# Turning attention's probabilities through DRAM (VectorE's 32x32 blocks, GpSimd's stores, a reload) in place of TensorE transposes

## The chip, the cores and the metric

The kernel runs on one core of a Trainium2 chip. The metric is the device time in microseconds of one execution. A run's time is a little longer than the span of its profile, which goes from the first instruction of the program to the last.

## The reference

One layer of a hybrid decoder is computed in float32 for a prompt of 1024 tokens and for 8 samples of 4 tokens each. The input is normalised and modulated, then multiplied by one wide matrix. Two branches follow: an mLSTM with 4 heads (a matrix memory, worked in chunks of 128 tokens) and a sliding-window attention with 8 query heads, 2 key heads, a head size of 64, a window of 128 and a learned sink per head. Gates merge the branches, an output matrix and a residual follow, and a last normalisation. The change touches the attention of the prompt alone:

```python
def sink_attend(q, k, v, q_pos, k_pos, sinks):
    ...
    s = jnp.einsum('bnqkgd,bnskd->bnkgqs', qg, k.astype(f32)) * (A_HEAD_DIM ** -0.5)
    ...
    s = jnp.where(mask[None, :, None, None], s, -jnp.inf)
    ...
    mx = jnp.maximum(jnp.max(s, axis=-1, keepdims=True), sink)
    p = jnp.exp(s - mx)
    den = jnp.sum(p, axis=-1, keepdims=True) + jnp.exp(sink - mx)
    o = jnp.einsum('bnkgqs,bnskd->bnqkgd', p / den, v.astype(f32))
```

Each block of 128 queries attends to the 128 keys of its own block and the 128 of the block before.

## The kernel before

**The main stream.** TensorE works through a list of jobs: the projections of keys and values, then four query groups (`aq`), eight inputs of the mLSTM heads (`mq`, `mk`, `mv` of heads 0 and 1 and two of head 2), and after them paired products (`block_products`) for the rest of the wide matrix: the other head inputs, the branch gates, the gates of attention and of the heads. The output matrices come last. Operands are split into a high and a low part, and each 128x128 step is three matmuls. The weights of a job are loaded one or two jobs ahead through SyncE's queue.

**The side streams.** All else that is computed meanwhile is written as Python generators that a planner, `Side`, weaves into the matmuls while the program is built. It keeps a clock, `side.now`, that each matmul moves on by its planned time. A generator issues some instructions and then yields a lag and the PSUM banks that its next step needs; the step is placed when the lag is over and the banks (`a`, `b`, `o`) have been left alone long enough (`HOLD`), and steps that need banks keep 1.5 us apart from the last one that issued products (`quiet`). The order on TensorE is fixed by this; on the chip the engines then wait for each other by semaphores. If an operand is late there, the whole of TensorE's queue stands behind it. Each stream has a limit of generators that are live at once and a least gap between their starts: `m` (the gate computations, then one generator `head(h)` per mLSTM head) 2 and 35 us; `a` (turning keys and values, then the 16 attention units) 5 and 8 us; `x` (sums of blocks for the paired products, loads) 2; `s` (attention of the samples, then `sample_head(h)`, four of them, added when head 3 has ended) 1; `g` 1. Where the main stream may not go on before side work has been placed, `hook` calls `side.until`: the first paired product waits for `sum_blocks`, the gates of attention for all 16 units (`units_done`), and the gate of head h, at its product 6, for sample head h.

**A unit.** `unit(g, b0)` (lines 806 to 874) is the attention of query group g (one query head of each of the 2 key heads) for the two query blocks b0 and b0 + 1. Queries, rotated keys and values come from DRAM (`qD`, `kD`, `vnD`), into two tiles `uqv` and `ukv` that also hold the values. Its steps are: load; scores into two banks and, on VectorE, mask and maximum into `p` (queries on the partitions, up to 256 keys by 2 blocks for each key head); the exponentials on ScalarE; the scaling by 1/den, for one key head on VectorE and for the other on ScalarE; the turn of `p`, so that keys come to the partitions, as six (in the units with b0 = 0) or eight transposes of 128x128 on TensorE into bank `b` and two copies back into `p`, one on ScalarE and one on VectorE; the product with the values into bank `o`; a copy and a store into `oD`. Between them stand lags of 12, 2.5, 3, 7 and 5 us.

**Two places that turn data in another way.** `across` (line 1021) turns keys and values of the mLSTM heads, and `stage_c3` (line 1118) the outputs of the heads: VectorE's `transpose` turns each 32x32 block in place, and four DMAs issued by GpSimd, one for 32 partitions, store the blocks so that the DRAM tensor holds the whole turned tile. Each run of such a store is 32 numbers, 128 bytes.

**Tiles.** Almost all of the streams' tiles in SBUF, 2 KB a partition, come from one pool of 43 (`ht`). All loads and stores of the side streams, the weights among them, go through SyncE's queue in the order in which they were written; stores are put off by 4 us of the planner's clock (`store`).

Of the kernel before, what the change touches and what calls it, by code (L numbers as in the profile page):

```python
# [111 lines left out]
class Side:  # L112
# [4 lines left out]
    def __init__(self, each, limits, quiet):  # L117
        self.each, self.free = each, {}
        self.now, self.last, self.quiet, self.products = 0.0, 0.0, quiet, 0
        self.streams = {n: {"max": m, "gap": g, "wait": [], "live": [], "next": 0.0} for n, (m, g) in limits.items()}  # L120

# [17 lines left out]
    def tick(self):  # L139
        self.each()  # L140
        for st in self.streams.values():
            if st["wait"] and len(st["live"]) < st["max"] and self.now >= st["next"]:
                self.begin(st)
        used, visit = set(), self.now >= self.last + self.quiet
        for item in sorted((i for st in self.streams.values() for i in st["live"]), key=lambda i: i[1]):
            banks = set(item[2])
            if self.now < item[1] or used & banks or (banks and not visit) or any(self.now < self.free.get(b, 0) for b in banks):
                continue
            used |= banks
            for b in banks:  # L150
                self.free[b] = self.now + (6.0 if "+" in banks else HOLD[b])
            n = self.products
            self.step(item)
            if self.products > n:
                self.last = self.now
# [17 lines left out]
def body(tc, a):  # L173
    nc = tc.nc
    with ExitStack() as ctx:
# [65 lines left out]
        def dma(out, in_, late=False):  # L241
            stores(in_.tensor)
            issue(out, in_, late)

        def issue(out, in_, late=False):
            ins = nc.sync.dma_start(out, in_)
            ins = getattr(ins, "ins", ins)
            if late:
                no_sync(ins, free)
                free.clear()  # L250
            free.append(ins)

        side = Side(stores, {"m": (2, 35.0), "a": (5,8.0), "x": (2, 0.0), "s": (1, 0.0), "g": (1, 0.0)}, 1.5)
        def mm(out, lhsT, rhs, start, stop, share=1, more=False):
# [552 lines left out]
        def unit(g, b0):  # L807
            sink = at["sink"]
            los = [128 if b == 0 else 0 for b in (b0, b0 + 1)]
            n0 = 1 if b0 == 0 else 0  # L810
            qv, kv_ = ht([128, 4, 128], "uqv"), ht([128, 4, 128], "ukv")
            q, kT = qv[:, 0:2].rearrange("p c e -> p (c e)"), kv_[:, 0:3].rearrange("p c e -> p (c e)")
            vn = kv_[:, 3], qv[:, 2], qv[:, 3]
            dma(q, qD[g][:, b0 * 128:b0 * 128 + 256])
            dma(kT[:, n0 * 128:], kD[:, (b0 - 1 + n0) * 128:(b0 + 2) * 128])
            dma(qv[:, 2:4], vnD[:, b0:b0 + 2])
            if b0:
                dma(vn[0], vnD[:, b0 - 1])
            yield 12.0, sc_bank[1]
            p = [ht([128, 2, 256], f"p{kv}") for kv in range(2)]  # L820
# [25 lines left out]
            for kv in range(2):  # L846
                for i, lo in enumerate(los):
# [3 lines left out]
                    else:  # L851
                        V.tensor_scalar(p[kv][:, i, lo:], p[kv][:, i, lo:], den[:, j:j + 1], None, op0=ALU.mult)
            yield 7.0, "b"
            pT = [t.rearrange("p i (j e) -> p (i j) e", e=128) for t in p]
            for kv in range(2):
                pt = pb([128, 4, 128], f"pt{g}_{b0}_{kv}")
                for j in range(n0, 4):
                    tr(pt[:, j], p[kv][:, j // 2, j % 2 * 128:j % 2 * 128 + 128], ident)
                if kv:
                    V.tensor_copy(pT[kv][:, n0:], pt[:, n0:])  # L860
                else:
                    S.copy(pT[kv][:, n0:], pt[:, n0:])
            yield 5.0, "o"
            oT = po([128, 2, 128], f"oT{g}_{b0}")
            for j in range(n0, 4):
                i, hf = divmod(j, 2)
                for kv in range(2):
                    r = slice(64 * kv, 64 * kv + 64)
                    mm(oT[r, i], vn[i + hf][:, r], pT[kv][:, j], start=(hf == 0 or b0 + i == 0), stop=(hf == 1))
            c0 = b0 * 128  # L870
            o = qv[:, 0:2].rearrange("p c e -> p (c e)")
            S.copy(o, oT.rearrange("p c e -> p (c e)"))
# [148 lines left out]
        def across(h, n, src, c0):  # L1021
            m = src.shape[1]
            t = ht([128, 512], f"{n}t")[:, :m]
            V.transpose(t, src)
            for b in range(0, 128, 32):
                nc.gpsimd.dma_start(mN[n][h][c0:c0 + m, b:b + 32].rearrange("(t p) e -> p t e", p=32), t[b:b + 32].rearrange("p (t e) -> p t e", e=32))  # L1026

        def head(h):
# [89 lines left out]
            def stage_c3(p):  # L1118
# [7 lines left out]
                for b in range(4):  # L1126
                    nc.gpsimd.dma_start(yhD[h][c0:c0 + m].rearrange("c (q i) (b e) -> b i c q e", i=32, e=32)[b], by_block(y[32 * b:32 * b + 32]))  # L1127

# [606 lines left out]
        def hook(n, i):  # L1735
# [11 lines left out]
            if (n, i) == (len(pairs) - 1, 7):  # L1747
                prefetch(("w_ao", 0))
                gated(("w_ao", 0))

        LOADS = [(len(pairs) - 2, 7), (len(pairs) - 1, 6), (len(pairs) - 1, 7)]
        work = block_products(pairs, hook)
# [387 lines left out]
```

## Time and profile before

| | us |
|---|---|
| median of 3 runs | 859.94 |
| lowest and highest of them | 857.38, 860.94 |
| the profiled execution | 857.75 |
| its span | 855.9 |

In that span TensorE is busy for 822.3 us, VectorE for 604.1, ScalarE for 390.5 and GpSimd for 174.7; the mean granted TensorE clock is 0.992. The scores of the first unit start at 94.9 us, the product with values of the last unit at 274 us.

In the profile, PE is TensorE's matmuls and PEld its weight loads, DVE is VectorE, ACT ScalarE, POOL GpSimd, SP SyncE (SPq, its issuing of DMAs). A row of instructions by tile has the line, the engine, the operation, the tile written and the tiles read, the number of instructions, the duration of one in ns (least, median, most), the first and the last start in us, and the shapes. Most instructions carry the line of a helper (L219 for VectorE and ScalarE, L258 for matmuls, L263 for transposes, L246 for SyncE's DMAs), so the tile names tell them apart: `sc` are the scores, `p` the probabilities, `pt` the transposes in PSUM, `oT` the product with values. Rows of stages have the start and end, the length, the busy time of each engine with its number of instructions, the granted clock, the busy share of the 16 DMA engines and the GB/s that they moved.

### The profile page before, as it was taken

The numbers are of one execution on the slowest core, as the hardware profiler recorded it, in microseconds if no ns is written. First come the engines' busy times: TensorE is split into PE (matmuls) and PEld (weight loads), VectorE is DVE, ScalarE is ACT, GpSimd is POOL, SyncE is SP. The second block draws the span as 40 slices with busy tenths as digits, with TensorE's granted clock in tenths as the row PEclk, the third lists the DMA queues.
The fourth block names the chain that finished last, engine by engine and source line by source line (L and its number), as shares of the span: only waits on it lengthen the run. The fifth ranks groups of instructions, "written<-read, shape, count | busy, mean of one in ns | idle before, by whom it ended". The sixth has DMA issues, their size and how long they took to land. (4 is left out here: it accounts for less than half of the span.)

```text
span 855.9 us, 15332 instructions
## 1 busy us (share of the span) xinstructions
PE 822.3 (96%) x5139; PEld 686.6 (80%) x5139; DVE 604.1 (71%) x1596; ACT 390.5 (46%) x963; POOL 174.7 (20%) x236
## 2 busy tenths in 40 slices
PE   6899999999999989999999999999999999999984
PEld 3689988789789778888887777777788999967863
DVE  3787785555687778668666565978766669857987
ACT  4672356545564543555444454434443333233334
POOL 0220000330341434211111000000012032532563
PEclk9999999999999999999999999999999999999998
DMA  9995549459756765664444335553436974273322
GB/s 326 366 356 183 150 137 291 134 125 294 214 153 203 214 170 151 194 198 135 129 115 130 115 111 162 160 150 89 116 99 203 345 254 137 82 247 99 111 99 104
DMA packets 125347, 150.82 MB, mean 176 GB/s; under 512 B 29057, under 2 KB 81409, under 8 KB 125237
## 3 DMA queue, kind: packets, MB, share of 16 engines
q1 hardware_dynamic: 121044, 143.55, 53.5%
q0 software_dynamic: 4224, 6.30, 3.6%
q8 instruction: 40, 0.66, 0.3%
q14 instruction: 39, 0.31, 0.1%
HBM read 109.73 MB, written 41.08 MB: 176 GB/s over the span
## 5 line engine op out<-in xcount | busy, mean ns | idle before, releaser
L1127 POOL DMA_DIRECT2D yhD<-yt x48 | 28.9, 608 | 108.3 <-DVE yt L219 86.3
L258 PE MATMUL g_w_ao<-ya,wh_w_ao 128*128 128x384 f32 (+1 forms) x192 | 45.7, 322 | 0.1
L258 PE MATMUL g_w_mo<-ym_l,wh_w_mo 128*128 128x384 f32 (+1 forms) x192 | 45.7, 323 | 0.0
L219 ACT ACTIVATE p<-p,nmx 128x256 f32<-128x256 f32 (+1 forms) x64 | 31.0, 486 | 28.3 <-DVE nmx L219 28.3
L1026 POOL DMA_DIRECT2D mkN<-mkt x44 | 26.9, 618 | 45.5 <-DVE mkt L219 26.0
L219 DVE CUSTOM_DVE_ANT_0 p<-sc,cst,sink 128x256 f32<-128x256 f32 (+1 forms) x64 | 26.1, 463 | 11.4 <-PE sc L258 11.4
L258 PEld LDWEIGHTS g_w_ao<-ya,wh_w_ao 128*128 128x128 f32 x192 | 33.5, 188 | 0.7 <-DVE ya L219 0.6
L258 PEld LDWEIGHTS g_w_mo<-ym_l,wh_w_mo 128*128 128x128 f32 x192 | 33.5, 188 | 0.0
L258 PE MATMUL g_aq<-h_h,wh_aq 128*128 128x384 f32 (+1 forms) x96 | 32.5, 338 | 0.0
L1026 POOL DMA_DIRECT2D mvN<-mvt x40 | 24.7, 624 | 33.6 <-DVE mvt L219 12.5
L258 PE MATMUL g_aq<-h_l,wh_aq 128*128 128x384 f32 (+1 forms) x96 | 31.0, 323 | 0.0
L258 PE MATMUL g_w_mo<-ym_l,wl_w_mo 128*128 128x384 f32 (+1 forms) x96 | 31.0, 323 | 0.0
L258 PE MATMUL g_aq<-h_h,wl_aq 128*128 128x384 f32 (+1 forms) x96 | 31.0, 323 | 0.0
L258 PE MATMUL g_w_ao<-ya,wl_w_ao 128*128 128x384 f32 (+1 forms) x96 | 30.8, 321 | 0.0
L258 PE MATMUL g_mq<-h_h,wh_mq 128*128 128x384 f32 (+1 forms) x72 | 24.7, 344 | 0.8 <-ACT vs L219 0.8
L258 PE MATMUL g_mk<-h_h,wh_mk 128*128 128x384 f32 (+1 forms) x72 | 24.8, 344 | 0.0
L219 POOL TENSOR_TENSOR ya<-yr,ya 128x384 fp32r<-128x384 f32 (+1 forms) x6 | 7.3, 1222 | 80.7 <-DVE hg L219 67.4
L258 PE MATMUL g_mk<-h_l,wh_mk 128*128 128x384 f32 (+1 forms) x72 | 23.2, 323 | 0.0
L258 PE MATMUL g_mk<-h_h,wl_mk 128*128 128x384 f32 (+1 forms) x72 | 23.2, 323 | 0.0
L258 PE MATMUL g_mq<-h_h,wl_mq 128*128 128x384 f32 (+1 forms) x72 | 23.2, 322 | 0.0
L258 PE MATMUL g_mq<-h_l,wh_mq 128*128 128x384 f32 (+1 forms) x72 | 23.2, 322 | 0.0
L219 POOL COPY qs<-mk 128x32 f32<-128x32 f32 x3 | 1.4, 463 | 103.1 <-ACT mk L219 103.1
(1700 smaller groups left out, 2800.9 us busy)
## 6 DMA issues: line engine op xcount, KB each, us to landing
hb<-hD SPq DMA_DIRECT2D x24, 256.0 KB
x<-xT SPq DMA_DIRECT2D x16, 256.0 KB
early_h<-w_ada SPq DMA_DIRECT2D x8, 512.0 KB
hD<-x SPq DMA_DIRECT2D x16, 256.0 KB
adar_ga<-w_ada SPq DMA_DIRECT2D x16, 256.0 KB
wr_ga<-w SPq DMA_DIRECT2D x16, 256.0 KB
wr_gm<-w SPq DMA_DIRECT2D x16, 256.0 KB
taD<-gt SPq DMA_DIRECT2D x16, 256.0 KB
```

The source lines that it names most:

```text
L219: ins = f(*args, **kw)
L258: in_order(nc.tensor.matmul(out, lhsT, rhs, start=start, stop=stop, skip_group_check=more))
L1026: nc.gpsimd.dma_start(mN[n][h][c0:c0 + m, b:b + 32].rearrange("(t p) e -> p t e", p=32), t[b:b + 32].rearrange("p (t e) -> p t e", e=32))
L1127: nc.gpsimd.dma_start(yhD[h][c0:c0 + m].rearrange("c (q i) (b e) -> b i c q e", i=32, e=32)[b], by_block(y[32 * b:32 * b + 32]))
```

## The change

The transposes on TensorE and the copies out of PSUM go. Once `p` is scaled, the unit turns the 32x32 blocks of each key head's half with one VectorE instruction, into the tiles that held queries and keys (now `uq` and `uk`), and stores them with four GpSimd DMAs for each key head into a DRAM tensor `pD`, as `stage_c3` does. Some 12 us of the planner's clock later, SyncE loads `pD` into two new tiles `pT0` and `pT1`, and the values, which were loaded with the queries before, into `uv`. The product with the values follows and is the same as before; its copy goes into `pT0`. The lags of a unit are now 9, 2.5, 3, 3, 12 and 5, where 9, 12 and 5 are the least: `landed` makes them longer when the planner's count of DMAs issued on that queue (0.42 us each on SyncE, 0.65 on GpSimd) says that the queue is behind. Bank `b` is no longer used by units. The gap of stream `a` is 6.5 instead of 8 us. A new table `held` keeps stream `m` from starting a generator while another of it is live and fewer than 16 units are done. The stores of `across` and `stage_c3` go through the new `scatter`, which issues the same DMA and counts it.

```diff
@@ Side.tick
-        for st in self.streams.values():
-            if st["wait"] and len(st["live"]) < st["max"] and self.now >= st["next"]:
+        for name, st in self.streams.items():
+            held = name in self.held and self.held[name]()
+            if st["wait"] and not held and len(st["live"]) < st["max"] and self.now >= st["next"]:
                 self.begin(st)
@@ body
+        queue = {"sync": 0.0, "gpsimd": 0.0}
+
+        def put(eng, cost):
+            queue[eng] = max(queue[eng], side.now) + cost
+
+        def landed(eng, least):
+            return max(least, queue[eng] - side.now + (2.5 if eng == "sync" else 4.0))
+
+        def scatter(out, in_):
+            nc.gpsimd.dma_start(out, in_)
+            put("gpsimd", 0.65)
+
         def issue(out, in_, late=False):
             ins = nc.sync.dma_start(out, in_)
+            put("sync", 0.42)
...
-        side = Side(stores, {"m": (2, 35.0), "a": (5,8.0), "x": (2, 0.0), "s": (1, 0.0), "g": (1, 0.0)}, 1.5)
+        side = Side(stores, {"m": (2, 35.0), "a": (5, 6.5), "x": (2, 0.0), "s": (1, 0.0), "g": (1, 0.0)}, 1.5)
@@ unit
-            qv, kv_ = ht([128, 4, 128], "uqv"), ht([128, 4, 128], "ukv")
+            qv, kv_ = ht([128, 4, 128], "uq"), ht([128, 4, 128], "uk")
             q, kT = qv[:, 0:2].rearrange("p c e -> p (c e)"), kv_[:, 0:3].rearrange("p c e -> p (c e)")
-            vn = kv_[:, 3], qv[:, 2], qv[:, 3]
+            pD = [dp.tile([4, 128, 128], F32, name=f"pD{g}_{b0}_{kv}") for kv in range(2)]
             dma(q, qD[g][:, b0 * 128:b0 * 128 + 256])
             dma(kT[:, n0 * 128:], kD[:, (b0 - 1 + n0) * 128:(b0 + 2) * 128])
-            dma(qv[:, 2:4], vnD[:, b0:b0 + 2])
-            if b0:
-                dma(vn[0], vnD[:, b0 - 1])
-            yield 12.0, sc_bank[1]
+            yield landed("sync", 9.0), sc_bank[1]
...
-            yield 7.0, "b"
-            pT = [t.rearrange("p i (j e) -> p (i j) e", e=128) for t in p]
+            yield 3.0, ""
+            flat = lambda t: t.rearrange("p c e -> p (c e)")
+            for kv, t in enumerate((qv, kv_)):
+                V.transpose(flat(t)[:, n0 * 128:], flat(p[kv])[:, n0 * 128:])
+                for k in range(4):
+                    scatter(pD[kv][n0:].rearrange("c (q i) (k e) -> k i c q e", i=32, e=32)[k],
+                                        by_block(flat(t)[32 * k:32 * k + 32])[:, n0:])
+            yield landed("gpsimd", 12.0), ""
+            pT = [ht([128, 4, 128], f"pT{kv}") for kv in range(2)]
+            vn = ht([128, 4, 128], "uv")
             for kv in range(2):
-                pt = pb([128, 4, 128], f"pt{g}_{b0}_{kv}")
-                for j in range(n0, 4):
-                    tr(pt[:, j], p[kv][:, j // 2, j % 2 * 128:j % 2 * 128 + 128], ident)
-                if kv:
-                    V.tensor_copy(pT[kv][:, n0:], pt[:, n0:])
-                else:
-                    S.copy(pT[kv][:, n0:], pt[:, n0:])
-            yield 5.0, "o"
+                dma(pT[kv][:, n0:], pD[kv][n0:].rearrange("c p e -> p c e"))
+            dma(vn[:, n0:3], vnD[:, b0 - 1 + n0:b0 + 2])
+            yield landed("sync", 5.0), "o"
             oT = po([128, 2, 128], f"oT{g}_{b0}")
...
-            o = qv[:, 0:2].rearrange("p c e -> p (c e)")
+            o = flat(pT[0][:, 0:2])
@@ across (stage_c3 likewise)
-                nc.gpsimd.dma_start(mN[n][h][c0:c0 + m, b:b + 32].rearrange("(t p) e -> p t e", p=32), t[b:b + 32].rearrange("p (t e) -> p t e", e=32))
+                scatter(mN[n][h][c0:c0 + m, b:b + 32].rearrange("(t p) e -> p t e", p=32), t[b:b + 32].rearrange("p (t e) -> p t e", e=32))
@@ main stream
+        side.held["m"] = lambda: len(side.streams["m"]["live"]) > 0 and len(units_done) < 16
```

More of the change, by code (lines that the diff above doesn't have):

```diff
@@ L119, in __init__ @@
         self.now, self.last, self.quiet, self.products = 0.0, 0.0, quiet, 0
+        self.held = {}
         self.streams = {n: {"max": m, "gap": g, "wait": [], "live": [], "next": 0.0} for n, (m, g) in limits.items()}
@@ L868, in unit @@
                     r = slice(64 * kv, 64 * kv + 64)
-                    mm(oT[r, i], vn[i + hf][:, r], pT[kv][:, j], start=(hf == 0 or b0 + i == 0), stop=(hf == 1))
+                    mm(oT[r, i], vn[:, i + hf, r], pT[kv][:, j], start=(hf == 0 or b0 + i == 0), stop=(hf == 1))
             c0 = b0 * 128
-            o = qv[:, 0:2].rearrange("p c e -> p (c e)")
+            o = flat(pT[0][:, 0:2])
             S.copy(o, oT.rearrange("p c e -> p (c e)"))
@@ L1126, in stage_c3 @@
                 for b in range(4):
-                    nc.gpsimd.dma_start(yhD[h][c0:c0 + m].rearrange("c (q i) (b e) -> b i c q e", i=32, e=32)[b], by_block(y[32 * b:32 * b + 32]))
+                    scatter(yhD[h][c0:c0 + m].rearrange("c (q i) (b e) -> b i c q e", i=32, e=32)[b], by_block(y[32 * b:32 * b + 32]))
             for visit in ([(load, 0), 10.0, ""], [(prep, 0), 3.0, "o"], [(stage_e, 0), (stage_a, 0), 5.0, "o"],
```

## The prediction

> **What bounds the kernel now.** I read the page's busy shares first, then the busy time by stage, then the rows of the work that goes.
>
> ```profile
> span 855.9 us, 15332 instructions
> PE 822.3 (96%) x5139; PEld 686.6 (80%) x5139; DVE 604.1 (71%) x1596; ACT 390.5 (46%) x963; POOL 174.7 (20%) x236
> q1 hardware_dynamic: 121044, 143.55, 53.5%
> q0 software_dynamic: 4224, 6.30, 3.6%
> ```
>
> TensorE is busy 96% of the span. The last two lines are the DMA queues of SyncE and of GpSimd: packets, MB, share of 16 engines.
>
> ```profile
> core 0: us, PE busy (x) PEld busy (x) DVE busy (x) ACT busy (x) POOL busy (x), PEclk, DMA share, GB/s
> 0.00:65.00 65.00, 55.01 (x364) 37.75 (x367) 42.92 (x113) 39.72 (x67) 11.42 (x24) 1.00 0.97 347
> 85.00:205.00 120.00, 119.18 (x901) 104.27 (x900) 76.76 (x294) 61.28 (x197) 15.43 (x26) 1.00 0.61 179
> 205.00:285.00 80.00, 78.48 (x599) 69.45 (x598) 57.77 (x182) 42.22 (x128) 27.01 (x46) 1.00 0.71 199
> 285.00:310.00 25.00, 21.53 (x130) 17.59 (x129) 19.29 (x69) 12.34 (x34) 7.38 (x14) 0.93 0.78 223
> ```
>
> The attention units run between 85 and 285 us. There TensorE idles 2.3 of 200 us, so time taken out of its queue is time saved, as long as nothing that it then needs comes late. VectorE is busy 134.5 of the 200, ScalarE 103.5, GpSimd 42.4.
>
> **The change, part by part.**
>
> *The turn on TensorE goes.* Its rows, the waits of TensorE in this stage, and one visit in order of time:
>
> ```profile
> L263 PE MATMUL pt<-cst,p x120: 270/272/331, 111.2 to 260.4; 128*128 128x128 f32 x120
> L219 DVE COPY p<-pt x16: 539/684/692, 112.3 to 260.7; 128x512 f32<-128x512 f32 x12, 128x384 f32<-128x384 f32 x4
> L219 ACT COPY p<-pt x16: 458/568/595, 112.6 to 261.5; 128x512 f32<-128x512 f32 x12, 128x384 f32<-128x384 f32 x4
> ...
> PE bx L258 <- DVE f3r_w L219: 2.3, 1, 2.3
> PE pt L263 <- ACT p L219: 1.5, 2, 0.8
> PE bw L258 <- DVE t2l L219: 1.2, 1, 1.2
> ...
> 111.05 0.34 PE L258 MATMUL g_aq<-h_h,wl_aq 128*128 128x384 f32 x1
> 111.22 0.82 PE L263 MATMUL pt<-cst,p 128*128 128x128 f32 x6
> 111.80 0.42 PE L258 MATMUL g_aq<-h_h,wh_aq 128*128 128x384 f32 x1
> 112.06 0.34 PE L258 MATMUL g_aq<-h_l,wh_aq 128*128 128x384 f32 x1
> ```
>
> A transpose has a duration of 272 ns, but they are pipelined, so 120 x 0.272 = 32.6 us would count each more than twice. What one visit takes from the queue is read from the starts: the projection's matmuls follow each other every 0.17 us; six transposes hold the next one from 111.22 to 111.80, and its follower comes after 0.26 instead of 0.17. That is 0.58 + 0.09 = 0.67 us for six, 0.11 each, and 120 x 0.112 = 13.4 us in 16 visits. The 1.5 us in which the transposes waited for ScalarE's scaling of p go as well. Gain on TensorE: **14.9 us**. The copies out of PSUM leave ScalarE (16 x 0.57 = 9.1 us) and VectorE (16 x 0.68 = 10.9); neither bounds the stage, so I count nothing for them.
>
> *The blocks turned on VectorE.* 32 more instructions; the rows of the same operation and of the stores behind it are in the kernel already:
>
> ```profile
> L219 DVE STREAM_TRANSPOSE mkt<-mk x9: 439/570/580, 149.0 to 282.9; 128x384 f32<-128x384 f32 x6, 128x256 f32<-128x256 f32 x3
> L219 DVE STREAM_TRANSPOSE mkt<-mkv x2: 703/703/703, 329.6 to 337.7; 128x512 f32<-128x512 f32 x2
> L1026 POOL DMA_DIRECT2D mkN<-mkt x44: 582/617/782, 149.9 to 341.1; - x44
> mvN<-mvt POOLq DMA_DIRECT2D x16, 64.0 KB, 4.4
> mkN<-mkt POOLq DMA_DIRECT2D x24, 48.0 KB, 3.0
> ```
>
> 24 at 0.70 and 8 three-quarter ones at 0.57 make 21.4 us; less the 10.9 of the copies VectorE gets 10.5 us more work in a stage where it idles 65. Hidden, with one exception. Six of the 16 turns start after 205 us; their units put 6 x 0.65 = 4 us ahead of the block operands for the paired products, and at 285 to 310 TensorE already waits for VectorE (bx 2.3, bw 1.2 us above), while its own work up to there gets 6 x 0.9 = 5.4 us shorter. Between 0 and 5.4 us of the gain is lost at this edge; I take **2**, nearer to nothing because one of the two heads that share VectorE there is held back (below).
>
> *GpSimd's stores.* Eight per unit, 128 in all, 128 x 0.617 = 79 us of issue in a stage where GpSimd is free for 158 of 200. They share its queue with the key and value stores (four at a time, 2.5 us); a unit's store that comes behind them is late by that, and they by 4.9 us behind a unit's eight; their readers are loads planned far later. Hidden.
>
> *The new path of the operands.* Its stations come from these rows (scores, scaling, products; the two times after each row's durations are its first and last start):
>
> ```profile
> L258 PE MATMUL sc<-ukv,uqv x128: 272/376/481, 94.9 to 243.2; 64*128 64x256 f32 x112, 64*128 64x128 f32 x16
> L219 DVE TENSOR_SCALAR p<-p,den x32: 286/348/519, 102.2 to 251.0; 128x256 f32<-128x256 f32 x28, 128x128 f32<-128x128 f32 x4
> L258 PE MATMUL oT<-p,uqv x192: 272/273/324, 118.0 to 274.1; 128*64 128x128 f32 x192
> ```
>
> The first unit's scores start at 94.9 and its p is scaled 7.3 us later. From there: one transpose 0.7, eight issues 4.9, landing 3 to 4.4 (median rows above), so, with 0.9 for the scaling itself, the turned blocks are in DRAM 17 to 18 us after the scores, up to 21 behind other stores. The reload is two DMAs of 256 KB; the page gives no landing for SyncE's queue. The nearest rows are the 64 KB ones of GpSimd's, 4.4, and the transfer itself at 199 GB/s is 2.6 us, so I take 4 to 9. Operands ready: 21 to 30 us after the scores, say 25. The order of work places the products at 2.5 + 3 + 3 + 12 + 5 = 25.5 plus a wait for an "o" bank; that wait was, with a lag of 5, between 111.2 and 118.0 in the first unit 1.8 us and between 260.4 and 274.1 in the last 8.7, so about 5. The products stand at 30, the operands come at 25 with a spread of some 4: about one unit in eight waits, for 2 to 3 us, 0.3 us on the mean of 16. Cost **5 us** in all; between none and 16 x 4 = 64 if every operand comes at 29.5 and no bank is waited for. Behind a waiting product stands all of TensorE's queue, the projections above all, so each such microsecond counts whole. SyncE's queue waits for the stores before it issues the reload; behind it stand the next unit's loads, weights and the loads of block operands, which then start late by the same microseconds. It is issued 12 us after the transposes, when the chain above takes 9 to 10; I count nothing unless GpSimd has a backlog.
>
> The unit's loads lose one DMA (values come in one piece, and late), and the scores follow after 9 instead of 12 us. No TensorE wait for scores stands among those of before, so 3 us less margin is covered; bound 0 to 16 x 1, taken as nothing. At its end a unit holds three more tiles (the reloaded p and the values) of the 43 that all streams share, but gives back the two of p a dozen microseconds earlier; taken as nothing too.
>
> *DMA traffic.* The stores write 7.86 MB and the reloads read as much. By the share per MB of the two queue lines, 3.6/6.30 of 855.9 us and 53.5/143.55, the stores take 38 us of all sixteen engines and the reloads 25. The stage holds 0.61 x 120 + 0.71 x 80 = 130 us of packets now; 193 would be in 185. But packet times include standing behind others, and in bytes it is 37.4 + 15.7 = 53.1 MB in 185 us, 287 GB/s, where the first 65 us carried 347. Crowded, not full: I count it in the 5 us above. The Trainium skill, "DMA: Bandwidth & Descriptors", Specifications, says that a transfer needs at least 512 bytes for line rate and that below this the engine reads, modifies and writes. The trace agrees in direction: GpSimd's queue, whose stores are runs of 128 bytes, pays 78 us of packet time per MB against 51; had the stores cost what SyncE's do, they would be 25 us instead of 38.
>
> *The order of work.* The "m" stream now holds a second head while one is live and not all 16 units are done. Lags of a unit sum to 34.5 us against 29.5, but one bank wait of three is gone, so a unit lives about as long as before, and five still run side by side: I expect the 16th to end 0 to 10 us after its old place less the gain, 260 to 269.
>
> ```profile
> 250.56 1.39 SPq L246 DMA_DIRECT2D hq<-qD  x1
> 354.71 0.45 SPq L246 DMA_DIRECT2D hq<-qD  x1
> L219 DVE STREAM_TRANSPOSE yt<-et x12: 438/572/579, 246.3 to 450.0; 128x384 f32<-128x384 f32 x8, 128x256 f32<-128x256 f32 x4
> L263 PE MATMUL sty<-cst,sns x4: 242/243/244, 493.3 to 622.0; 32*128 32x32 f32 x4
> 640.13 0.39 PE L258 MATMUL bw<-t2h,wh_phead_gate__7542 128*128 128x512 f32 x1
> ```
>
> Head 1 started its loads at 250.56; its end let head 3 start at 354.71, which ended at 450; then the four sample heads follow one another and the last ends at 622.0. The last pair's product at 640.13 may not be placed before that: 18 us of slack. The gain moves 640 to about 632, so head 1 may be 10 us late. At 260 to 269 it is 9 to 18 late; without units beside it a head runs quicker. I take **1 us** lost, 0 to 8.
>
> *Sum:* the profiled execution took 857.75 us (1.9 outside the span); 857.75 - 14.9 + 2 + 5 + 1 = **850.9 us**. That execution is 2.2 below the median of the runs shown, and within their spread; I give 851.
>
> **Rivals.**
>
> *A. The operands come late in most units.* At 0.9 us per unit (landing 7 instead of 4, or SyncE behind its own waits) the gain is used up: 850.9 + 16 x 0.6 = 860.5, no change. For it: the longest landing on GpSimd's queue was 7.0 us. Against it: the "o" bank's wait gives 5 us of margin.
>
> ```profile
> DMA to landing us min/median/max: 2.0/3.6/7.0
> ```
>
> *B. The DMA engines fill up; slower.* Place: 85 to 285. If the packet times add as they stand, 193 us are needed, and at the highest share that a ten-microsecond window of the unit stage reached, 0.92 (below), the stage takes 210 instead of 200: 857.75 + 10 = 868. It decides as soon as the added traffic costs over 54 us by the packets' time (0.92 x 200 - 130). Against it: 347 GB/s was moved in the first stage.
>
> ```profile
> 135.00:145.00 10.00, 10.00 (x89) 8.95 (x86) 6.17 (x24) 6.16 (x19) 0.43 (x1) 1.00 0.92 301
> ```
>
> *C. The heads are held too long.* If the units end after head 0, head 1 starts about 40 us late, 30 of which reach 640: some 880.
>
> *D. GpSimd can't issue beside VectorE.* If each store had first to let one VectorE instruction of the length of a transpose pass, a unit's eight took 8 x (0.62 + 0.70) = 10.6 us instead of 4.9. The operands came at 31 us, behind the products at 30, and with the spread of 4 the mean wait were 2.1: 850.9 + 16 x 1.8 = 880. The trace speaks against it: the 44 key stores took 582 to 782 ns each, with VectorE 64 to 72% busy around most of them. The Trainium skill, "SBUF — State Buffer", Who interferes with whom, states such a lock (a store of GpSimd takes some 620 ns alone and 3100 beside a VectorE copy in a two-port mode). By that figure a unit's eight would take up to 25 us; no row here shows it.
>
> **How the numbers follow.** A measurement of this kernel tells about 0.5% (4.3 us) from no change. My forecast, 842 to 855: 0.60. A: 0.18. B: 0.10. C: 0.07. D: 0.03. Better than 842 (no waits at all, 843, and the wait at 285 gone too): 0.02. Faster 0.62, same 0.18, slower 0.20. The range 842 to 868 leaves out the better case, half of B, C and D, some 0.17; the likeliest case alone is 842 to 855.
>
> **What would show it.** Right: no transposes of p on TensorE, 32 more stream transposes near 0.7 us, 128 more GpSimd stores near 0.62, and TensorE's waits before the products with values summing to about 5 us; 285 us of before's work reached near 275. Wrong: those waits over 10 us (A); DMA share above 0.9 through the stage and waits on weights or block operands (B); TensorE idle near 630 ahead of the last pair (C). My weakest numbers are the reload's landing time and the end of the sixteenth unit.

## The result: 5% slower, and the profile after

The changed kernel takes 903.09 us (median of 4 runs, 901.48 to 908.11), the kernel before 859.5 beside it: 1.0519 times as long, 95% interval 1.0469 to 1.0569. The forecast was 851, with 868 as the upper end of its range. The profiled execution took 901.48 us.

The page of the changed kernel (lines as those shown of before):

```profile
span 899.7 us, 15403 instructions
PE 828.4 (92%) x5019; PEld 688.4 (77%) x5019; DVE 617.5 (69%) x1612; ACT 383.5 (43%) x947; POOL 254.5 (28%) x364
q1 hardware_dynamic: 135188, 151.42, 54.0%
q0 software_dynamic: 8320, 14.17, 7.1%
```

The 120 transposes are gone (5139 matmuls became 5019), 128 GpSimd instructions are new, and TensorE is busy for 6 us more than before: the same matmuls last longer. Its busy time and clock by stage:

```profile
85.00:205.00 120.00, 106.65 (x739) 91.70 (x739) 74.04 (x279) 49.23 (x163) 64.52 (x104) 0.93 0.79 211
205.00:285.00 80.00, 61.27 (x392) 51.23 (x391) 46.28 (x155) 33.17 (x109) 37.51 (x61) 0.87 0.80 227
285.00:310.00 25.00, 22.53 (x176) 21.00 (x175) 14.30 (x39) 8.27 (x24) 13.49 (x23) 0.93 0.81 214
```

Of the 200 us from 85 to 285 TensorE now idles 32 (before 2.3), and its granted clock has fallen from 1.00 to 0.93 and 0.87. The first paired product (`bx`), at 282.3 us before, starts at 320.7: 38 of the 44 us are lost by then. What it waits for between 85 and 330 us (total, times, longest):

```profile
PE oT L273 <- DMA uv<-vnD: 33.0, 9, 7.2
PE g_mq L273 <- DVE mvt L221: 5.0, 2, 3.2
PE g_mq L273 <- ACT mk L221: 0.4, 1, 0.4
PE oT L273 <- DMA qD<-mk: 0.2, 1, 0.2
```

33 us are the product with values waiting for its reloaded operands. The clock comes on top. Two short stretches of the changed kernel, each at or behind such a wait, and the only one of before in this part of the run:

```profile
136.80:143.60 6.80, 3.14 (x21) 2.84 (x22) 0.00 (x0) 0.37 (x1) 4.55 (x8) 0.50 1.08 346
280.10:283.50 3.40, 3.40 (x19) 2.96 (x19) 1.51 (x9) 2.54 (x11) 3.40 (x7) 0.50 0.60 189
```

```profile
302.40:305.80 3.40, 3.40 (x13) 2.93 (x12) 3.40 (x10) 1.24 (x2) 2.19 (x4) 0.50 0.84 245
```

The clock in them is 0.50. Between 85 and 330 us the changed kernel has nine such stretches of 3.4 or 6.8 us, one at or behind each of its nine waits of 1.8 us or more, and none by the two of 1.2 us. So such a wait is paid for again in part. The Trainium skill, "TensorE: Matmul & The Clock Gate", HAM oscillation, describes waits on DMAs that put the clock back to half; by its Part 1 that goes in windows of about 3.4 us, and the lengths here agree with it. The Trainium skill puts the limit there at idle gaps of about 3.4 us; here five waits of 1.8 to 3.2 us were enough.

What the clock costs is read from TensorE's busy time up to the first paired product (the rows 85.00:282.30 and 85.00:320.70 further below): an estimated 13.4 us of transposes are gone, and yet it is 2.0 us longer (196.97 against 194.96), so the slow stretches cost about 15. Together, 38.6 us of waits against 2.3 before and these 2.0 make 38, and the product is 38 late.

Why the operands come late is seen in one unit, in order of time (the changed kernel's timeline, engine by engine):

```profile
254.38 0.71 DVE L221 STREAM_TRANSPOSE uq<-p 128x512 f32<-128x512 f32 x1
255.02 0.67 DVE L221 STREAM_TRANSPOSE uk<-p 128x512 f32<-128x512 f32 x1
...
268.93 2.44 POOL L256 DMA_DIRECT2D mvN<-mvt  x4 [9.64 <-DVE mvt L221]
271.35 2.58 POOL L256 DMA_DIRECT2D pD<-uq  x4
273.93 2.57 POOL L256 DMA_DIRECT2D pD<-uk  x4
...
284.36 0.32 SPq L260 DMA_DIRECT2D oD<-pT  x1
284.86 0.98 SPq L260 DMA_DIRECT2D pT<-pD  x2
285.89 0.49 SPq L260 DMA_DIRECT2D uv<-vnD  x1
...
290.52 1.76 PE L273 MATMUL oT<-pT,uv 128*64 128x128 f32 x14 [2.22 <-DMA uv<-vnD]
```

The blocks are turned at 255.7; GpSimd stores them from 271.35, because in its queue they stand behind a value store that itself waited 9.6 us for VectorE; SyncE reloads them at 284.86, behind the store of the unit before (`oD`), which waits for that unit's product; and the product starts 4.6 us after the reload's last issue, 2.2 of them in TensorE's idle time. Three queues, each in a fixed order, take turns waiting for each other.

### The profile page after: what moved, and what is told of

It reads as the page before. It is cut to its first block, busy times and chain, and to the rows that moved or that the text cites. A ratio compares the mean times of both kernels' runs of the same rounds, so it can differ in the third digit from the quotient of the medians.

```text
span 899.7 us, 15403 instructions
## 1 busy us (share of the span) xinstructions
PE 828.4 (92%) x5019; PEld 688.4 (77%) x5019; DVE 617.5 (69%) x1612; ACT 383.5 (43%) x947; POOL 254.5 (28%) x364
## 5 line engine op out<-in xcount | busy, mean ns | idle before, releaser
L256 POOL DMA_DIRECT2D pD<-uq x64 | 40.8, 644 | 54.2 <-DVE uq L221 39.8
L273 PE MATMUL oT<-pT,uv 128*64 128x128 f32 x240 | 23.0, 349 | 33.3 <-DMA uv<-vnD 33.0
L273 PEld LDWEIGHTS oT<-pT,uv 128*64 128x64 f32 x240 | 18.2, 178 | 37.8 <-issue 27.8
L256 POOL DMA_DIRECT2D pD<-uk x64 | 41.0, 647 | 1.9 <-DMA mkN<-mkt 1.4
L273 PE MATMUL g_mq<-h_h,wh_mq 128*128 128x384 f32 (+1 forms) x72 | 27.4, 380 | 5.4 <-DVE mvt L221 5.0
L273 PE MATMUL g_mq<-h_l,wh_mq 128*128 128x384 f32 (+1 forms) x72 | 25.3, 352 | 0.0
```

Source lines behind the costliest of these rows:

```text
L256: nc.gpsimd.dma_start(out, in_)
L273: in_order(nc.tensor.matmul(out, lhsT, rhs, start=start, stop=stop, skip_group_check=more))
```

## The experiments

The theories, with the numbers or letters that the texts quoted below use: (1) the product stands too close behind its reload; (2) the added traffic; later split into (2a, then b) the DMA engines are full, runs of 128 bytes above all, (2b, then a) GpSimd's queue is late, with all that stands in it, (2c) SyncE's queue has two more issues of a unit ahead of other loads, and (c) SyncE's queue stands behind GpSimd's stores; (3) the order of work has changed. Where a kernel's product "reads the turned tiles in SBUF", the right operands are left out and the matmuls are as many and as large as before; where no load fills the tiles `pT`, these are left out too. Times are medians, intervals are of the ratio to before, which took 858.8 to 859.5 beside them.

### The place of the product, and the order (four runs)

e1, the product 12 instead of 5 us behind the reload:
```diff
-            yield landed("sync", 5.0), "o"
+            yield landed("sync", 12.0), "o"
```


> The changed kernel with one number other: the product with values is placed 12 us of the planner's clock behind the reload instead of 5. Theory 1 (the product stands in TensorE's queue at about the moment at which SyncE issues the reload; each wait then costs itself and a stretch at half the granted clock): the waits before the products fall from 33 us to under 6, the half-clock stretches of the unit stage go with them, and the time comes to 850 to 865. Theory 2 (the DMA engines are full, so that more lag only moves the wait): over 20 us of TensorE waits remain on loads and the time stays within 12 us of 903. Theory 3 (the order of work, the held heads above all, makes the loss): 895 to 915.

e2, stores and reloads as they are, the product reads the turned tiles:
```diff
-  mm(oT[r, i], vn[:, i + hf, r], pT[kv][:, j], ...)
+  mm(oT[r, i], kv_[:, i + hf + 1, r], (qv, kv_)[kv][:, j], ...)
-  o = flat(pT[0][:, 0:2])
+  o = flat(qv[:, 0:2])
```


> The changed kernel, but the product reads the block-turned tiles in SBUF (for the probabilities and in place of the values), so it waits for no reload; blocks, stores and reloads all still run. This leaves the right operands of the attention's product out. Theory 1: no waits before the products, the clock whole, 845 to 858. Theory 2: the traffic is the same, weights and block operands come late instead, over 885. Theory 3: over 885 too, since the placing is the same.

e3, the kernel before with the gap of 6.5 and the held head alone:
```diff
# and the test of `held` in Side.tick
-        side = Side(... "a": (5,8.0) ...)
+        side = Side(... "a": (5, 6.5) ...)
+        side.held["m"] = lambda: len(side.streams["m"]["live"]) > 0 and len(units_done) < 16
```


> The kernel before with the new gap of 6.5 us for units and the holding of the head stream, and nothing else of the change. Theories 1 and 2: 850 to 870, near the kernel before. Theory 3: over 880, most of the loss.

e4, the changed kernel without the held head (the last line above taken out):

> The changed kernel without the holding of the head stream. Theory 1: products wait as before, 890 to 920. Theory 2: as theory 1 or some us worse, since more loads fall into the stage. Theory 3: under 885.

Measured: e1 912.5 (1.0589 to 1.0636), e2 898.36 (1.0429 to 1.0485), e3 860.82 (1.0005 to 1.0035), e4 901.49 (1.046 to 1.0509). TensorE's waits from 85 to 330 us in e1, then in e2:

```profile
PE g_mv L273 <- ACT mk L221: 7.8, 1, 7.8
PE oT L273 <- DVE mx L221: 7.2, 1, 7.2
PE sc L273 <- DMA uk<-kD: 6.3, 3, 5.2
...
PE oT L273 <- DMA uv<-vnD: 4.2, 1, 4.2
```

```profile
PE sc L273 <- DMA uk<-kD: 10.5, 4, 4.4
PE gp L273 <- ACT adas_ga L221: 9.9, 1, 9.9
PE g_mq L273 <- ACT mk L221: 6.6, 2, 6.2
```

e1's stage from 85 us to the first paired product, and its longest wait, which comes behind that (from 285 to 345 us):

```profile
85.00:303.20 218.20, 186.89 (x1308) 162.96 (x1306) 137.48 (x482) 92.64 (x299) 111.31 (x181) 0.93 0.79 221
PE bx L273 <- DVE mvt L221: 12.6, 1, 12.6
```

Theory 1 falls as the cause of the whole: with the wait for the reload pushed back or taken away, the time hardly changes, because other things then come late: the loads for the scores, the copies out of PSUM, or a result of ScalarE (`adas_ga` in e2, whose queue had stood 6.1 us for the load of a head's keys). It has a part, though. In e1 the wait for the reload falls from 33.0 to 4.2 us and the first paired product starts 17.5 us sooner than in the changed kernel; behind it the run loses 28 us more than the changed kernel does, 12.6 of them in one wait for VectorE, whose queue had itself stood 5.9 us for a DMA. The longer lag without the held head was not run. e1's 912.5 lies in the ranges of theories 2 and 3, but only 10.5 us of its waits are for loads, where theory 2 said over 20. Theory 3 falls as well, by e3 and e4: the order alone costs 1.5 us, and without the hold the changed kernel stays where it is.

### Traffic part by part (four runs)

f1 is e2 without stores and reloads, the planner's counts kept; the others add to it.
```diff
# f1
-  scatter(pD[kv][n0:]...[k], by_block(flat(t)[32 * k:32 * k + 32])[:, n0:])
+  put("gpsimd", 0.65)
-  dma(pT[kv][:, n0:], pD[kv][n0:].rearrange("c p e -> p c e"))
+  put("sync", 0.42)
# f2: f1 with the stores.   f3: f1 with loads of that size and those runs from an input
# f4: e2, each of the 128 rows stored and reloaded as one run of 2 KB
-  scatter(pD[kv][n0:].rearrange("c (q i) (k e) -> k i c q e", i=32, e=32)[k], ...)
+  scatter(pD[kv]...rearrange("(p x) -> p x", p=128)[32 * k:32 * k + 32, n0 * 128:], flat(t)[32 * k:32 * k + 32, n0 * 128:])
```


> As the run in which the product reads the turned tiles in SBUF, and neither the stores of the turned blocks nor their reloads are issued (the planner counts them as before, so the order of work is the same; the right operands of the product are left out). Theory 2 (traffic: the DMA engines or a queue are full, and loads of scores' operands and weights come late): 840 to 852, the gain that was forecast. Theory 3 (the order of work or VectorE's transposes): over 885, unchanged. If it lies between, both have a part.

> The same with the stores issued and no reloads. Theory 2a (the DMA engines' time is the limit): the stores have more packet time (7.1% against 3.6% of 16 engines' span, 30 us) than the reloads, so 865 to 885. Theory 2b (GpSimd's queue: its stores come up to 16 us late and hold their tiles, for which loads on SyncE then wait): 885 to 900, all of the loss. Theory 2c (SyncE's queue, with two more issues of a unit in front of the others' loads): under 860.

> The same with no stores, and two loads of the same size and runs of 512 bytes, from the output matrix instead of the stored blocks, in the reloads' place. Theory 2a: 860 to 880. Theory 2b: under 855. Theory 2c: 885 to 900.

> Stores and reloads both, product from the turned tiles, but every row of a store and of a reload is one run of 2 KB in DRAM instead of runs of 128 and 512 bytes (the order of the blocks is left out). Theory 2a: the short runs make the packets dear; 860 to 880. Theories 2b and 2c: as with the short runs, 890 to 903.

Measured: f1 853.67 (0.9908 to 0.9957), f2 876.58 (1.0174 to 1.0303), f3 854.75 (0.993 to 0.9969), f4 862.1 (1.0011 to 1.0061). Against f1, the reloads alone cost 1 us, the stores alone 23, both in whole rows 8, both as they are (e2) 45. f2 and f4 lie in the ranges of theory 2a; f3 misses its 860 to 880 and lies in theory 2b's (under 855). f1 is 1.7 us above the range of theory 2; f6, below, shows what it still loses.

The two queues between 85 and 285 us (packets, MB, share of 16 engines) in f1, f2, f3 and f4:

```profile
q1 hardware_dynamic: 29229, 35.43, 58.7%
q0 software_dynamic: 2176, 3.02, 7.2%
```
```profile
q0 software_dynamic: 6108, 10.71, 26.3%
```
```profile
q1 hardware_dynamic: 44612, 42.84, 71.4%
```
```profile
q0 software_dynamic: 6082, 10.67, 17.3%
```

The stores in runs of 128 bytes cost (26.3 - 7.2)% of 200 = 38.2 us of all engines for 7.7 MB, the reloads (71.4 - 58.7)% = 25.4; in whole rows the same stores cost 20.2. So f2 and f4 take the same packet time in all, with 7.9 MB more moved by f4. The Trainium skill's sentence on transfers below 512 bytes ("DMA: Bandwidth & Descriptors", Specifications), on record in the prediction, agrees with this in direction. The stage from 85 us to the first paired product, for before, f1, f3, f4, f2, e2 and the changed kernel (the last columns are clock, DMA share, GB/s):

```profile
85.00:282.30 197.30, 194.96 (x1487) 171.50 (x1485) 132.13 (x470) 103.11 (x324) 40.30 (x68) 1.00 0.65 187
```
```profile
85.00:271.70 186.70, 184.22 (x1362) 159.82 (x1360) 138.37 (x485) 93.95 (x301) 39.38 (x68) 0.99 0.65 192
```
```profile
85.00:273.80 188.80, 183.88 (x1353) 159.45 (x1351) 137.72 (x482) 93.57 (x301) 39.76 (x68) 0.98 0.77 230
```
```profile
85.00:276.60 191.60, 185.18 (x1350) 160.13 (x1348) 134.79 (x477) 93.26 (x300) 98.97 (x189) 0.97 0.85 262
```
```profile
85.00:281.50 196.50, 183.33 (x1352) 158.27 (x1350) 137.77 (x481) 93.11 (x300) 119.43 (x195) 0.98 0.82 220
```
```profile
85.00:315.50 230.50, 195.39 (x1354) 167.92 (x1352) 137.90 (x478) 93.22 (x302) 116.45 (x189) 0.92 0.80 220
```
```profile
85.00:320.70 235.70, 196.97 (x1351) 169.96 (x1349) 141.67 (x484) 93.64 (x301) 118.82 (x192) 0.91 0.80 220
```

Share times length is the packet time in the stage: 128 us before, then 121, 145, 163, 161, 184 and 189. TensorE could do the stage in 187 (f1). At 145 it is held up by 2 us, at 161 to 163 by 5 and 10, at 184 by 44. That is the direction of theory 2a: the loss grows steeply where the packet time reaches the length of the stage. e2 and f4 differ in one edit, how the rows lie in DRAM, and 36 of the 45 us go with it.

What theory 2a doesn't explain are the 14 us of run time between f2 and f4 at the same packet time. 4.9 of them lie in the stage (196.5 against 191.6 us). Right behind it f2 has its longest wait, from 284.8 to 294.2 us, and f4 none like it:

```profile
PE n L273 <- ACT uq L221: 9.9, 2, 9.4
```

A product of a head (`n`) waits for the copy of a unit's result (`uq`), which stands in ScalarE's queue behind work that waits for the load of the head's keys and for VectorE's operands of the paired products. ScalarE is thus a fourth queue in a fixed order. In f4 a store also takes GpSimd less long (498 against 648 ns, medians of `pD<-uq`), so theory 2b stayed in play. In e2 and the runs built on it that copy also writes over `uq`, which GpSimd's stores read, so it has to follow them, unlike in the changed kernel; between 85 and 330 us ScalarE waited for a DMA there for 3.5 us at most (f4).

### Less traffic, a queue without traffic, no hold, one group alone (four runs)

```diff
# g2: the changed kernel, one in eight of the weight tiles of the layer's last gate loaded
+                    if k < 1:
                         raws.append(ht([128, 512], f"adar_ga{j}{k}"))
                         dma(raws[-1], a["w_ada"][4 + j, :, k])
+                    else:
+                        raws.append(raws[0])
# g3: f1 with stores of 16 bytes a row and block
+  scatter(pS[kv][32 * k:32 * k + 32]..., t[32 * k:32 * k + 32, n0:4, 0:4])
# f6: f1 without the held head
-  side.held["m"] = lambda: ...
# h1: before, with the four units of group 0 alone turned through DRAM
#     (lags 12, 14, 12; gap 8; no held head)
```


> The changed kernel, stores and reloads as they are, but of the weights of the attention's gate (the jobs that run between about 215 and 320 us) only one tile in eight is loaded, so about 3.5 MB less go through SyncE's queue in the attention stage; this leaves out those weights' values. TensorE's work, the order of work and the turn of the probabilities are those of the changed kernel. Theory 'the DMA engines are full': some 14 us of packet time of all 16 engines leave a stage that needed 188 and had 187 without stretching, so the loss against the kernel without stores and reloads falls by 15 to 25 us: 880 to 890. Theory 'GpSimd's queue is late, and so the reloads': the chain of each unit is what it was, 900 to 906.

> The kernel without stores and reloads (product from turned tiles in SBUF), plus GpSimd's eight stores per unit cut to 16 bytes a row: the queue, the issue times and the waits of GpSimd are there, the bytes are not (some 0.2 MB instead of 7.9). It leaves out the right operands of the product. Theory 'the DMA engines are full': within 3 us of the kernel without them, 851 to 858. Theory 'GpSimd's queue holds back what stands behind it (key and value stores of the mLSTM heads, whose readers are then late)': at least half of the 23 us that the whole stores alone cost, 865 or more.

> The kernel without stores and reloads (853.7), and without the rule that holds the second head back. It asks where the 10.6 us that this kernel had won when the paired products begin were lost again by its end (2.4 left). If the held head costs them: 846 to 850. If they are lost at the edge where TensorE waits for VectorE's block operands, whatever the heads do: 851 to 856.

> The kernel before, with the turn through DRAM for the 4 units of the first query group alone; the other 12 units turn on TensorE as before; no head is held back, the gap between units is the old 8, and the lag between the reload and the product is 12 instead of 5. The first units run between 95 and 165 us. Theory 'the DMA engines are full': a quarter of the traffic (4 MB, some 15 us of packet time spread over 70) fits, 4 x 0.84 + some waits saved: 855 to 858. Theory 'the reload's way is too long for this place in any case': waits of 2 to 4 us in each of the four units, 863 to 872.

Measured: g2 907.56 (1.0548 to 1.0584), g3 874.08 (1.0163 to 1.0206), f6 845.33 (0.9834 to 0.988), h1 862.97 (1.0026 to 1.0058).

g2's weights are those of `ada_ga`, whose products run from 167 to 239 us, and not, as the text quoted says, the attention gate's. Its stage:

```profile
85.00:324.90 239.90, 195.06 (x1337) 169.45 (x1335) 139.22 (x480) 93.41 (x301) 116.87 (x189) 0.90 0.74 196
```

g2 speaks against theory 2a alone: the packet time in the stage was 0.74 x 239.9 = 178 us, 11 less than in the changed kernel, and the product waited for its reload as before (36.6 us in all). As long as the chain of three queues sets the pace, some relief of the engines buys nothing; and e2 showed that with the product out of that chain, the loss is nearly as large.

g3 was to have no traffic. The queues of the whole execution in f1 and in g3:

```profile
q1 hardware_dynamic: 119316, 143.55, 53.2%
q0 software_dynamic: 4224, 6.30, 3.3%
```
```profile
q1 hardware_dynamic: 119316, 143.55, 56.3%
q0 software_dynamic: 8320, 6.55, 3.7%
```

The tiny stores add 0.25 MB; yet SyncE's packets, the same in number and bytes, took 56.3% of 871.0 instead of 53.2% of 853.5 us, 36 us more, where f1, f6 and k2, with the same packets on that queue, differ by 6. So g3 doesn't separate the theories: with these small writes the packets of the other queue last longer.

f6 shows the gain of the change, and what the hold costs without traffic: it is 8.3 us faster than f1, 0.7 below the range for the hold. From 285 to 345 us in f1, then f6:

```profile
285.00:345.00 60.00, 53.93 (x304) 43.64 (x302) 40.27 (x106) 25.91 (x66) 20.14 (x32) 0.94 0.62 181
```
```profile
285.00:345.00 60.00, 58.38 (x367) 47.73 (x366) 46.70 (x138) 28.59 (x73) 24.92 (x40) 1.00 0.67 176
```

The held head works after the units, beside the first paired products, where VectorE makes the block operands; without the hold TensorE is busy 4.5 us longer there, at full clock.

h1 lies between its two ranges, at the edge of the second, whose waits it doesn't have: the product waited for its reload 0.2 us in all, and still nothing was gained. Its longest waits are these, and the first fell at 255 us, where no unit goes through DRAM any more:

```profile
PE sc L259 <- DVE mx L220: 4.3, 1, 4.3
PE pt L264 <- ACT p L220: 2.7, 2, 2.1
```

A changed order of a few units, with a quarter of the traffic, can thus cost some microseconds far from them; so differences below about 10 us between these kernels carry a cause only where their rows show the place, as in f6.

### Who waits for GpSimd's stores (four runs)

```diff
# k1: f2, the mLSTM heads' keys and values loaded from an input (right ones left out)
-  dma(t, mN[n][h][c0:c0 + w]...)
+  dma(t, a["w_out"][c0:c0 + w, h * 128:h * 128 + 128]...)
# k2: f1, in place of each store
+  G.tensor_copy(flat(p[kv])[:, n0 * 128:], flat(t)[:, n0 * 128:])
# k3: e2, the reloads read an input
-  dma(pT[kv][:, n0:], pD[kv][n0:]...)
+  dma(pT[kv][:, n0:], a["w_out"][512 * kv:512 * kv + 512, ...]...)
# k4: k3 with k1's edit
```


> Stores alone (876.6; product from turned tiles, no reloads), but the mLSTM heads load their keys and values from an input of the same size and runs instead of from the tensors that GpSimd's key and value stores write; those stores still run. It leaves out the right keys and values of the heads as well. Theory a (key and value stores late behind the eight stores of a unit, their readers late): 854 to 862. Theory b (the engines' time that 128-byte runs take): the traffic is the same, 870 to 880.

> No stores and no reloads (853.7), but in place of each store GpSimd copies the turned tile inside SBUF, eight copies a unit of about 0.6 us, so its queue is as long as with the stores and no byte goes to DRAM. Theory a: the queue alone delays the key and value stores, 868 or more. Theory b: 852 to 858.

> Stores and reloads both, product from turned tiles (898.4), but the reloads read an input of the same size and 512-byte runs, so SyncE does not stand behind the stores. Theory c (SyncE held by the stores): the sum of stores alone and reloads alone, 875 to 881. Theory b (DMA time): 893 to 900, since the traffic is the same.

> As the last one, and the heads load keys and values from an input too: all traffic of the changed kernel and all of GpSimd's queue are there, and nobody waits for a store of GpSimd in the attention stage but the heads' outputs. Theories a and c together: 855 to 863. Theory b: 885 to 900.

Measured: k1 883.91 (1.027 to 1.0324), k2 871.66 (1.0116 to 1.0171), k3 889.2 (1.0326 to 1.0374), k4 891.22 (1.0345 to 1.0409).

k1 and k4: taking the heads off the stores buys nothing (k1 is 7 us slower than f2, above both ranges, and its `n` still waits 9.0 us), so late keys and values are not the cause. k3: when SyncE doesn't stand behind the stores, the stage takes 208.5 us, 22 us less than in e2 at nearly its packet time (0.89 x 208.5 = 186):

```profile
85.00:293.50 208.50, 189.01 (x1351) 162.76 (x1349) 135.82 (x478) 91.82 (x298) 119.85 (x193) 0.95 0.89 244
```

At the end 9 of these 22 us are left, since k3 loses 13 us more than e2 behind the stage, where its `n` waits 10.3 us. So theory c is half of the loss in the stage and a fifth of the 45 in all; the time lies between the ranges of c and b. k4, in which neither the reloads nor the heads wait for GpSimd's stores, still lies 37.5 us above f1, within what theory b expected. k2 misled: it came out 18 above f1 without a byte of traffic, but with its copies VectorE's work took longer, and ScalarE's copies into `uq` waited 7.6 us for them. The stage in k2 (third busy time: VectorE, 158.7 us, against 138.4 for the same work in f1):

```profile
85.00:286.90 201.90, 190.12 (x1356) 164.38 (x1354) 158.68 (x482) 93.68 (x301) 118.61 (x195) 0.95 0.62 176
```

### The stores on another queue, and whole rows without the hold (two runs)

```diff
# m1: f2, the same DMAs issued by SyncE
-  scatter(pD[kv][n0:]...[k], by_block(...))
+  store(pD[kv][n0:]...[k], by_block(...)); put("gpsimd", 0.65)
# m3: f4 without the held head
-  side.held["m"] = lambda: ...
```


> Stores alone (876.6; product from turned tiles, no reloads), the same DMAs of 128-byte runs, but issued by SyncE, some 4 us of the planner's clock after the transposes, like the other stores; GpSimd's queue is that of the kernel without them. It leaves out the right operands of the product. Theory 'GpSimd's queue': 853 to 862, with some microseconds for 128 more issues on SyncE. Theory 'runs of 128 bytes cost the engines their time, whoever issues them': 870 to 885.

> Stores and reloads with whole rows (862.1, product from turned tiles), without the rule that holds the second head. Without any stores and reloads the rule cost 8.3 us (853.7 against 845.3). If its cost adds to that of the traffic: 852 to 857, below the kernel before. If the traffic is what sets the end and the rule costs nothing beside it, as in the changed kernel itself (903.1 against 901.5): 859 to 863.

Measured: m1 896.71 (1.0378 to 1.0474), m3 860.58 (1.0 to 1.0037). Off GpSimd's queue the stores cost not less but more, 43 us above f1 and above both ranges. GpSimd's time is thus not needed for the loss. Nor is m1 a clean price of the runs, since it puts 128 issues of about 0.5 us into SyncE's own queue, ahead of the loads. m3 shows that with traffic the hold costs nothing that can be told (862.1 with it), and that even whole rows, whose blocks are not fully turned, don't get below before. No kernel with the turn through DRAM beat it.

## Why the prediction was wrong, point by point

- **Gain of 14.9 us, less 2 at the edge.** Right as a sum. f6 leaves just these two steps of the sum and has a span of 843.2, 12.7 below before; predicted 12.9. Its first paired product starts 12.6 us sooner than before, and nothing is lost behind it, so 12.6 of the 14.9 arrived and the 2 at the edge were not lost: that the sum fits is in part luck. The block transposes cost VectorE what was said (medians 708 and 670 ns).
- **"Crowded, not full: I count it in the 5 us above."** This is the step that failed. The prices under it were right: 38 and 25 us of packet time, measured 38.2 and 25.4. They summed to 193 us in a stage of 185, and I set that aside because in bytes it was 287 GB/s where another stage had carried 347. The stage of 85 to 285 us doesn't carry that with these runs: at a share of 0.80 the changed kernel moved 220 GB/s up to its first paired product, an estimated 275 at a full share. Rival B named the place and the condition (over 54 us of added packet time; 189 - 128 = 61 were added) but priced it as 10 us by dividing the need by the highest share. It cost 44 in e2's stage, where late transfers stop the queues of TensorE, ScalarE and SyncE in turn and the clock is halved behind TensorE's waits (mean 0.92). f1, without stores and reloads, shows that the traffic and the queues it stands in make all of the loss.
- **Products waiting, 5 us.** 33 measured. With the median landing of 4.2 us behind the last issue, the blocks of the first nine units were in DRAM 17 to 27 us after the scores began (predicted 17 to 21), those of the last seven 27 to 44: there GpSimd's queue held them ("nothing unless GpSimd has a backlog": it had one, 16 us in the unit shown), and SyncE's held the reload behind the store of the unit before. This is rival A's mechanism, and it explains the waits that the profile names; but e1 and e2 show that without them the time isn't won back.
- **GpSimd's stores, "Hidden".** Their issue took 648 ns in the median, near the 617 taken, and VectorE's presence didn't slow it (rival D fell). Yet alone they cost 23 us (f2), 10 in the stage and 11 behind it, which the step did not foresee.
- **The scores 3 us sooner, "taken as nothing".** Right for the changed kernel: no wait for `sc` stands in its list. In e1 and e2 the scores waited 6.3 and 10.5 us.
- **Heads held, 1 us (0 to 8).** Without traffic 8.3 us, mis-sized: the reason given for a small loss at the edge (one of two heads is held) was turned round, since the held head comes right there. In the changed kernel it didn't matter (e4).

What stays open is how the 45 us of e2 divide between full engines and queues that stand behind late transfers. Packet time alone doesn't tell: at 184 to 189 us the stage lost 22 us against f1 in k3, 44 in e2 and 49 in the changed kernel, and at 178 it lost 53 in g2. A packet's time also changes with what another queue does (g3), so it is no clean price of the work. Nor does any run show why f2's `n` waits and f4's doesn't. A turn with long runs both in the stores and in the reloads was not tried: the whole rows of f4 leave the blocks in their old places.

## What to carry to other kernels

Add up what new DMA traffic needs in packet time at the price of rows with the same run length, against the length of its own stage: when the sum comes near to the stage (here 178 to 189 of 187 us), work that looked hidden comes late everywhere, and removing any one of the waits only shows the next. Bytes per second reached in another stage, with other runs, are no bound for this one. Count the queues that a new path goes through, for each stands still behind its own late work. And a stall on TensorE is paid for again in part where the clock is halved behind it.

## What the runs showed of the hardware that was not expected

- In the changed kernel, at or behind all nine of TensorE's waits of 1.8 us or more the granted clock stood at 0.50 for 3.4 or 6.8 us; in e2 one wait of 2.1 us, at 160.6 us, had no such stretch behind it.
- 128-byte runs cost 5.0 us of all 16 engines per MB on GpSimd's queue, whole rows 2.6 (38.2 and 20.2 us for 7.7 MB).
- With stores of 0.25 MB in all, in tiny runs, the packets of SyncE's queue took 36 us more (g3); with copies on GpSimd VectorE was busy 20 us longer (k2), while with its DMA issues it was not (f2: 137.8 against 138.4 us in the stage).
